# Gate multiplications held back by one result, one block in its own buffer, squares summed in a bank, 15 low parts of w_up by ScalarE and adding transfers

## The chip, the cores and the metric

The kernel runs on one core of one Trainium2 chip. The metric is the device time of one execution in microseconds (us): the time before is 820.95 us, the median of three runs (820.51 to 821.41).

## The reference

One decoder layer on 512 tokens (T) of 1024 channels (D), all in float32:

```python
u = rmsnorm(x);  proj = u @ w_in        # glu, q, k, v, r, low-rank decay, gates A and B
c = silu(layernorm(causal_conv31(a * sigmoid(g))));   y_conv = c @ w_conv_out
o = gated_linear_attention(q, k, v, decay);  o = rmsnorm(o) * silu(r);  y_gla = o @ w_gla_out
h = x + (sigmoid(gate_a) * y_conv + sigmoid(gate_b) * y_gla) @ w_o
z = causal_conv3(rmsnorm(h) @ w_ffn_up)              # 2 x 2816 channels
out = rmsnorm(h + (silu(z_a) * z_b) @ w_ffn_down)
```

## The kernel before

**Products.** TensorE (PE) multiplies in a reduced float32 format, so every operand is split into a high part and a low part (`whi`, `wlo` for weights; `uh`, `ul` and other pairs for activations), and every product is three matmuls (`mm3`, lines 527 to 529; for w_up the first of the three reads `wlo`, the two others `whi`). The weights come in tiles of 128x1024 float32 (512 KB) by transfers from the SP queue into one of four `raw` buffers. `split_weight` then makes the parts, each from a ring of four buffers: ScalarE (ACT) copies `raw` into `whi` (lines 412 and 442). For `wlo` there are three ways:

- VectorE (DVE) subtracts `whi` from `raw` (lines 413 and 450);
- for tiles listed in `ADDED`, ACT writes `raw` times -1 rounded to the reduced format, into `wlo` (line 444), and a transfer from the POOL (GpSimd) queue that adds to its destination brings the same weights from DRAM once more (line 445), so that what the rounding left off stays in `wlo`;
- for two tiles, POOL subtracts.

**Order.** The program is one list of weight tiles (`order`), and `LOOK = 2` tiles are made ready ahead of the one in use. Some pairs of products are done with seven block products in place of eight ("two" and `SEVEN`): their operands are sums of weight blocks, which POOL makes with `two_sums` (line 384, parts x1 and x3) or DVE with line 360 (`kept`), and PE's partial results are put together by DVE (`r`, line 1535, or `tmp`, line 1335). Engines run their own instructions in the order in which the program gives them, and wait for each other at semaphores.

**Around the r gate (w_r, about 225 to 290 us).** The columns r of w_in go through the steps a11, a12, s1, n2, s4, n3, a22 (`seven`), each with two blocks d = 0 and 1. `put_r` takes each result out of PSUM: the first ones into `r` buffers (ring of 8), later ones by a DVE sum or difference in place (line 1535); when a result is final, ACT applies Silu (line 1536) and DVE multiplies it into the attention output `ot` (line 1537; in the profile `h<-h,r`, since `ot` lies in buffers of the name h). The last block of w_r, step a22 with d = 1, is loaded into a `raw` buffer (line 346); behind it in SP's queue are the two blocks of the first pair of w_gb (line 292), whose sums POOL makes.

**Around the LayerNorm of the convolution (about 310 to 335 us).** `ln_center(k)` for eight channel tiles subtracts the mean on DVE (line 1015, `c`), squares on ACT (line 1017) and adds the square to a running sum on DVE (line 1021). The running sum is in an SBUF buffer `btmp`. PSUM banks of the name ax are three.

**Feed-forward (about 465 us to the end).** w_up has 44 tiles; 28 of them are used plain (the numbers in the change are among theirs), 16 in eight pairs. The low parts of all plain tiles are made by DVE (line 450). POOL makes the pairs' sums (line 384), and from its queue go adding transfers for w_down (lines 350 and 374). ACT and DVE also take PE's results out of PSUM and do the width-3 convolution and the gate between them.

Of the kernel before, what the change touches and what calls it, by code (L numbers as in the profile page):

```python
# [10 lines left out]
F32 = mybir.dt.float32  # L11
# [4 lines left out]
ALU = mybir.AluOpType  # L16

P = 128
D = 1024
T = 512  # L20
NT = T // P
KT = D // P
# [24 lines left out]
ADDED = {("w_glu", j) for j in range(4, 2 * KT)} | {("w_qk", m) for m in range(KT)}  # L47
ADDED |= {("w_v", KT // 2 + j) for j in range(KT // 2)} | {("w_gb", m) for m in range(AHEAD)}
POOLED = {("w_qk", 0), ("w_qk", 1)}
ADDED -= POOLED  # L50
RATE = 5.0
ROWS = (0, 5, 5, 5, 8, 8, 8, 8)
EVERY = (6, 6, 6, 6, 4, 4, 4, 4)
# [47 lines left out]
def trunk_layer(ctx: ExitStack, tc: tile.TileContext, a: dict, out: bass.AP):  # L101
    nc = tc.nc
# [5 lines left out]
    def scoped(name, bufs, side="left"):  # L108
        scope = ExitStack()
        return scope, scope.enter_context(tc.tile_pool(name=name, bufs=bufs, side=side))  # L110
# [16 lines left out]
    def nm(s):  # L127
        return f"{s}_{next(names)}"
# [7 lines left out]
    def btmp():  # L136
        return tp.tile([P, T], F32, tag="btmp", name=nm("btmp"), bufs=2)
# [17 lines left out]
    def ax_bank():  # L155
        return ps.tile([P, T], F32, tag="ax", name=nm("ax"), bufs=3)
# [124 lines left out]
    def load():  # L281
        if len(raws) < len(order):
            name, j = order[len(raws)]
            if name in SEVEN:
                raws.append(load_block(name, *j))
                return
            if name == "two":
                name, p, q, part = j
                if part == "x1":
                    pair_raws[name, p] = [raw_tile() for _ in range(2)]  # L290
                    for raw, m in zip(pair_raws[name, p], (p, q)):
                        nc.sync.dma_start(raw, a[name][m])
                raws.append(None)
                return
            raw = raw_tile()
            nc.sync.dma_start(raw, a[name][j])
            raws.append(raw)
# [8 lines left out]
    def raw_tile():  # L306
        return wp.tile([P, D], F32, tag="raw", name=nm("raw"), bufs=4)


    def block(name, pairs, d, row, col):  # L310

        pairs = pairs[2 * d : 2 * d + 2]
        first = pairs[0][row]
        if name == "w_r":
            tiles = a[name][4 * col : 4 * col + 4, :, first * P : (first + 2) * P]
            return tiles.rearrange("m p c -> p m c")
        w = a[name][col * SEVEN[name] + first // 2]
        return w if len(pairs) == 2 else w[:, row * T : (row + 1) * T]

    def keep_tile(name):  # L320
        if name in ("w_o", "w_r"):
            return tp.tile([P, D], F32, tag="x", name=nm("kept"), bufs=3)
        return fp.tile([P, D], F32, tag="kept", name=nm("kept"), bufs=2)

    def shaped(name, t):
        return t.rearrange("p (m c) -> p m c", c=2 * P) if name == "w_r" else t
# [4 lines left out]
    def load_block(name, pairs, step, d):  # L331

        loads = R_LOADS if name == "w_r" else LOADS
        if step not in loads:
            return None
        at = loads[step]
        src = block(name, pairs, d, *at)
        n = D if name == "w_r" else src.shape[-1]
        if step == "a11":
            dst = keep_tile(name)[:, :n]  # L340
            kept[pairs, d] = dst
        elif (name, step, d) == ("w_r", "a22", 0):
            dst = keep_tile(name)
        else:
            dst = raw_tile()[:, :n]
        load_dma = nc.sync.dma_start(shaped(name, dst), src)
        if name == "w_down":
            tc.keep_in_program_order(load_dma)
        if step == "n3":
            nc.gpsimd.dma_start(dst, block(name, pairs, d, 1, 1), accum_op=ALU.add)  # L350
        if step in ("n2", "s1"):
            kept[pairs, d, "b22" if step == "n2" else "b12"] = dst
        return dst
# [100 lines left out]
    def prefetch(n):  # L454

        while len(ready) < min(used[0] + n, len(order)):
            split_weight()
# [10 lines left out]
    def weight(name, j, ahead=LOOK):  # L468
# [3 lines left out]
        prefetch(ahead)  # L472
        share = {"two": 2.5, "w_glu": RATE, "w_r": 2.0}.get(name, RATE)
        quiet[0] = name == "w_v"
        if name == "w_qk":
            share = 1.0 if j < 2 else RATE
        if name == "w_gb" and j > 3:
# [498 lines left out]
    stat = {}  # L976
# [36 lines left out]

    def ln_center(k):
        nc.vector.tensor_tensor(conv[k], stat["mean"], conv[k], ALU.add)
        sq = btmp()
        nc.scalar.activation(sq, conv[k], AF.Square)
        if k == 0:
            stat["sq"] = sq
        else:  # L1020
            nc.vector.tensor_tensor(stat["sq"], stat["sq"], sq, ALU.add)  # L1021

    def ln_var():
        v = small(NT, "mean")
# [27 lines left out]
    def norm_chain():  # L1052
        chain = [(RATE, ln_parts)]
        chain += [(2.5, lambda: None)] * 3
        chain.append((0, ln_mean))
        chain.extend((2, lambda k=k: ln_center(k)) for k in range(KT))
        chain += [(2.5, lambda: None)] * 4
        chain.append((RATE, ln_var))
        chain.append((2.5, lambda: None))
        chain.append((0, ln_rstd))  # L1060
        chain.extend((2.5, lambda k=k: ln_out(k)) for k in range(KT))
        return chain
# [164 lines left out]
    ot = {}  # L1227
# [180 lines left out]
    r_scope, rp_ = scoped("r", 8, "right")  # L1408
# [106 lines left out]
        def __getitem__(self, step):  # L1515
            return tuple(x[self.k] for x in merge_acts[step])

    rt = {}
    urgent += s4 + of_s4 + n3 + of_n3

    def sums_for(step):
# [2 lines left out]

    def put_r(step, t, n, acc):
        if step in ("a11", "s1", "n2"):
            rt[t, n] = rp_.tile([P, T], F32, tag="r", name=nm("r"), bufs=8)
            return nc.scalar.copy(rt[t, n], acc)
        if step == "a22":
            rt[t, n] = rp_.tile([P, T], F32, tag="r", name=nm("r"), bufs=8)  # L1530
            nc.scalar.activation(rt[t, n], acc, AF.Silu)
        else:
            r = rt[t, n]
            one, two = (r, acc) if step == "n3" else (acc, r)
            done = nc.vector.tensor_tensor(r, one, two, ALU.add if step == "a12" else ALU.subtract)
            nc.scalar.activation(r, r, AF.Silu)
        nc.vector.tensor_tensor(ot[t, n], ot[t, n], rt[t, n], ALU.mult)
        return done if step == "n3" else None

    def r_at(step, i):  # L1540
        if (step, i) == ("a22", 1):
            for m in range(4, KT):
                gated_o(m, ax_bank)

    seven("w_r", R_PAIRS, [ByTile(k) for k in range(4)], None, r_at, put=put_r, before=sums_for)
    half_of = [range(KT // 2), range(KT // 2, KT)]
    open_tiles = {}
# [282 lines left out]
    for gi, pairs in enumerate(GROUPS):  # L1830
# [26 lines left out]
        for what, i, *rest in up_plan(gi):  # L1857
# [7 lines left out]
            if what == "part":  # L1865
                if rest[0] == "x1":
                    units[i] = two_tiles("w_up", i, FT + i, lambda: up_acts, ax_bank)
                done = next(units[i])
# [112 lines left out]
```

## Time and profile before

| what | value |
|---|---|
| median of three runs | 820.95 us |
| the profiled execution | 821.88 us |
| its span, first to last instruction | 820.2 us |
| PE busy | 808.7 us (99%) |
| DVE busy | 707.2 us (86%) |
| ACT busy | 488.2 us (60%) |
| POOL busy | 196.8 us (24%) |
| granted clock of TensorE | 0.998 |

The profiled execution takes 821.88 us, of which 820.2 lie between its first and its last instruction and 1.7 around them. In the views, a row of a timeline has its start, its duration, the engine (an engine's name with q is its queue of transfers), the line, the operation and the tiles as out<-in; in brackets stands how long the engine was idle before it and what ended that. A row with x2 holds two neighbours of one kind. In the groups, the columns behind the bar are busy time, mean nanoseconds of one, and the idle time ahead of them. A matmul of 128x512 is shown with 0.39 to 0.40 us though the next starts 0.23 us behind it: they are pipelined, so starts are what to compare.

### The profile page before, as it was taken

To read this page: it belongs to the slowest core of one execution; us is meant where nothing else is said; L and a number is where in the kernel's file an instruction comes from. 1 tells how busy PE (TensorE), PEld (TensorE's weight loads), DVE (VectorE), ACT (ScalarE), POOL (GpSimd) and SP (SyncE) were. 2 spreads that over 40 slices of the span, in tenths; PEclk is the share of its full clock that TensorE was granted. 3 is DMA by queue.
4 is the path that set the end of the run, shared out by engine and by line. 5 is a ranking of instruction groups with operands and counts; after the bars stand their busy time and mean duration, and the time that the engine had idled before them with its cause. 6 is when DMAs were issued, how large, how long until landed. Compare 5 with 4: busy or idle time off the path is not lost.

```text
span 820.2 us, 11465 instructions
## 1 busy us (share of the span) xinstructions
PE 808.7 (99%) x4227; PEld 695.5 (85%) x4227; DVE 707.2 (86%) x1105; ACT 488.2 (60%) x744; POOL 196.8 (24%) x176
## 2 busy tenths in 40 slices
PE   9999999999999999999999999999999999999996
PEld 8888888888888788889988898898889988899885
DVE  6879999998999878595789889979975999689895
ACT  6667788677547574384445646556435663466554
POOL 2025433332203332122001100230123311522012
PEclk9999999999999999999999999999999999999999
DMA  8488858655831332433458613146632346335662
GB/s 327 153 193 177 190 161 178 157 123 134 183 96 36 96 111 95 129 103 103 155 106 227 201 58 103 52 159 166 140 130 92 143 121 167 103 103 178 156 129 103
DMA packets 36472, 113.60 MB, mean 139 GB/s; under 512 B 3688, under 2 KB 8944, under 8 KB 36416
## 3 DMA queue, kind: packets, MB, share of 16 engines
q1 hardware_dynamic: 28912, 86.39, 31.0%
q0 software_dynamic: 7488, 26.48, 18.9%
q8 instruction: 33, 0.54, 0.3%
q14 instruction: 23, 0.19, 0.1%
q10 hardware_dynamic: 16, 0.00, 0.0%
HBM read 110.76 MB, written 2.10 MB: 138 GB/s over the span
## 4 chain that ended last, share of the span: by engine, by line
PE 62%; DVE 1%; ACT 0%; issue 0%; POOL 0%; POOLq 0%; ACTq 0%
PE mm L527 14%; PE mm L528 14%; PE mm L529 14%; PE cv L527 4%; PE cv L528 4%; PE cv L529 4%; PE ax L529 2%; PE ax L527 2%; PE ax L528 2%; DVE btmp L1021 0%; PE ax L608 0%; PE ax L1233 0%; DVE wlo L413 0%; ACT junk L1778 0%; DVE hres L1485 0%
## 5 line engine op out<-in xcount | busy, mean ns | idle before, releaser
L527 PE MATMUL mm<-uh,wlo 128*128 128x512 f32 (+1 forms) x532 | 194.0, 365 | 0.7 <-DVE tmp L1335 0.7
L528 PE MATMUL mm<-ul,whi 128*128 128x512 f32 (+1 forms) x532 | 191.5, 360 | 0.0
L529 PE MATMUL mm<-uh,whi 128*128 128x512 f32 (+1 forms) x532 | 191.5, 360 | 0.0
L413 DVE TENSOR_TENSOR wlo<-raw,whi 128x1024 fp32r<-128x1024 f32 x82 | 96.8, 1186 | 30.4 <-ACT whi L412 26.6
L384 POOL TENSOR_TENSOR raw<-raw,raw 128x512 f32<-128x512 f32 x39 | 59.8, 1534 | 239.5 <-DVE wlo L413 107.3
L527 PEld LDWEIGHTS mm<-uh,wlo 128*128 128x128 f32 x532 | 100.5, 189 | 16.5 <-DVE tmp L1335 1.1
L529 PEld LDWEIGHTS mm<-uh,whi 128*128 128x128 f32 x532 | 100.4, 189 | 15.3
L528 PEld LDWEIGHTS mm<-ul,whi 128*128 128x128 f32 x532 | 100.5, 189 | 14.8
L442 ACT CAST whi<-raw 128x1024 fp32r<-128x1024 f32 x80 | 83.5, 1048 | 30.4 <-PE mm L529 13.3
L412 ACT CAST whi<-raw 128x1024 fp32r<-128x1024 f32 x82 | 78.9, 965 | 38.1 <-PE mm L529 23.1
L450 DVE TENSOR_TENSOR wlo<-raw,whi 128x1024 fp32r<-128x1024 f32 x50 | 66.2, 1328 | 7.2 <-ACT whi L442 7.1
L412 ACT CAST whi<-kept 128x1024 fp32r<-128x1024 f32 (+1 forms) x40 | 40.2, 1007 | 30.2 <-DVE kept L360 15.7
L413 DVE TENSOR_TENSOR wlo<-kept,whi 128x1024 fp32r<-128x1024 f32 (+1 forms) x40 | 47.9, 1201 | 5.5 <-ACT whi L412 5.5
L887 DVE SCALAR_TENSOR_TENSOR aside<-cv,pp,aside 128x255 f32<-128x255 f32 (+6 forms) x112 | 52.1, 465 | 0.0
L887 DVE SCALAR_TENSOR_TENSOR c<-aside,btmp,c 128x247 f32<-128x247 f32 (+13 forms) x93 | 52.0, 564 | 0.0
L887 DVE SCALAR_TENSOR_TENSOR c<-cv,pp,c 128x247 f32<-128x247 f32 (+13 forms) x93 | 43.2, 464 | 1.4 <-ACT c L883 1.4
L444 ACT ACTIVATE wlo<-raw 128x1024 fp32r<-128x1024 f32 x28 | 29.4, 1059 | 19.0 <-PE mm L527 19.0
L1332 ACT COPY tmp<-mm 128x256 f32<-128x256 f32 x38 | 14.1, 370 | 34.0 <-PE mm L529 33.4
L1705 DVE SCALAR_TENSOR_TENSOR tmp<-mm,pp,tmp 128x511 f32<-128x511 f32 (+1 forms) x42 | 31.0, 741 | 2.6 <-ACT tmp L1702 2.5
L1705 DVE SCALAR_TENSOR_TENSOR tmp<-tmp,pp,tmp 128x511 f32<-128x511 f32 (+1 forms) x32 | 27.8, 887 | 0.4
L384 POOL TENSOR_TENSOR raw<-raw 128x512 f32<-128x512 f32 x13 | 26.4, 2032 | 0.0
L1485 DVE TENSOR_TENSOR hres<-hres,mm 128x512 f32<-128x512 f32 (+1 forms) x37 | 24.6, 673 | 2.1 <-PE mm L529 2.0
(499 smaller groups left out, 2092.9 us busy)
## 6 DMA issues: line engine op xcount, KB each, us to landing
raw<-in_w_up_dram SPq DMA_DIRECT2D x44, 512.0 KB, 3.6
raw<-in_w_glu_dram SPq DMA_DIRECT2D x16, 512.0 KB, 5.3
raw<-in_w_down_dram SPq DMA_DIRECT2D x15, 512.0 KB, 4.1
wlo<-in_w_glu_dram POOLq DMA_DIRECT2D x12, 512.0 KB, 7.0
kept<-in_w_down_dram POOLq DMA_DIRECT2D x10, 512.0 KB, 6.2
raw<-in_w_v_dram SPq DMA_DIRECT2D x8, 512.0 KB, 5.8
raw<-in_w_qk_dram SPq DMA_DIRECT2D x8, 512.0 KB, 6.3
raw<-in_w_gb_dram SPq DMA_DIRECT2D x8, 512.0 KB, 4.5
```

The costliest lines, as they stand in the source:

```text
L384: work = nc.gpsimd.tensor_tensor(out, x, y, ALU.add)
L412: nc.scalar.copy(hi, raw)
L413: two_low[:] = [nc.vector.tensor_tensor(lo, raw, hi.bitcast(F32), ALU.subtract)]
L442: nc.scalar.copy(hi, raw)
L444: pace[0] = nc.scalar.mul(lo, raw, -1.0)
L450: pace[0] = nc.vector.tensor_tensor(lo, raw, hi.bitcast(F32), ALU.subtract)
L527: nc.tensor.matmul(acc, ll, rh, start=first, stop=False, **kw)
L528: nc.tensor.matmul(acc, lh, rl, start=False, stop=False, **kw)
L529: nc.tensor.matmul(acc, lh, rh, start=False, stop=last, **kw)
L887: nc.vector.scalar_tensor_tensor(out[:, j:], x[:, : half_t - j], w, out[:, j:], ALU.mult, ALU.add)
L1485: done = nc.vector.tensor_tensor(hres[t, n][:, c], hres[t, n][:, c], acc[:, c], op)
L1705: nc.vector.scalar_tensor_tensor(z[:, s:], acc[:, : T - s], w[j], z[:, s:], ALU.mult, ALU.add)
```

## The change

- **Gate multiplications.** `put_r` no longer issues `ot *= r` as soon as the Silu is asked for. It puts the pair into a list `gated`, and the next call issues it behind that call's DVE sum or difference. The last one (a22, t = 3) is issued at once. The ring of `r` goes from 8 to 6 buffers.
- **The last block of w_r** is loaded into a buffer of its own, `rx`, in place of a `raw` buffer.
- **Squares.** The running sum of squares starts in a bank of PSUM (`ax`), and only the last sum is written to `btmp`. The first square is written by ACT into the bank.
- **w_up.** 15 plain tiles go into `ADDED`: their `wlo` is made by ACT and an adding transfer, and no longer by DVE.

```diff
--- before.py
+++ after.py
@@ -48,6 +48,7 @@
 ADDED |= {("w_v", KT // 2 + j) for j in range(KT // 2)} | {("w_gb", m) for m in range(AHEAD)}
 POOLED = {("w_qk", 0), ("w_qk", 1)}
 ADDED -= POOLED
+ADDED |= {("w_up", j) for j in (1, 23, 3, 25, 4, 26, 8, 9, 31, 20, 35, 16, 39, 19, 41)}
 RATE = 5.0
 ROWS = (0, 5, 5, 5, 8, 8, 8, 8)
 EVERY = (6, 6, 6, 6, 4, 4, 4, 4)
@@ -341,6 +342,8 @@
             kept[pairs, d] = dst
         elif (name, step, d) == ("w_r", "a22", 0):
             dst = keep_tile(name)
+        elif (name, step, d) == ("w_r", "a22", 1):
+            dst = rp_.tile([P, D], F32, tag="rx", name=nm("rx"), bufs=1)
         else:
             dst = raw_tile()[:, :n]
         load_dma = nc.sync.dma_start(shaped(name, dst), src)
@@ -1013,12 +1016,14 @@
 
     def ln_center(k):
         nc.vector.tensor_tensor(conv[k], stat["mean"], conv[k], ALU.add)
-        sq = btmp()
+        sq = btmp() if k else ax_bank()
         nc.scalar.activation(sq, conv[k], AF.Square)
         if k == 0:
             stat["sq"] = sq
         else:
-            nc.vector.tensor_tensor(stat["sq"], stat["sq"], sq, ALU.add)
+            total = stat["sq"] if k < KT - 1 else btmp()
+            nc.vector.tensor_tensor(total, stat["sq"], sq, ALU.add)
+            stat["sq"] = total
 
     def ln_var():
         v = small(NT, "mean")
@@ -1515,7 +1520,7 @@
         def __getitem__(self, step):
             return tuple(x[self.k] for x in merge_acts[step])
 
-    rt = {}
+    rt, gated = {}, []
     urgent += s4 + of_s4 + n3 + of_n3
 
     def sums_for(step):
@@ -1524,17 +1529,26 @@
 
     def put_r(step, t, n, acc):
         if step in ("a11", "s1", "n2"):
-            rt[t, n] = rp_.tile([P, T], F32, tag="r", name=nm("r"), bufs=8)
+            rt[t, n] = rp_.tile([P, T], F32, tag="r", name=nm("r"), bufs=6)
             return nc.scalar.copy(rt[t, n], acc)
         if step == "a22":
-            rt[t, n] = rp_.tile([P, T], F32, tag="r", name=nm("r"), bufs=8)
+            rt[t, n] = rp_.tile([P, T], F32, tag="r", name=nm("r"), bufs=6)
             nc.scalar.activation(rt[t, n], acc, AF.Silu)
         else:
             r = rt[t, n]
             one, two = (r, acc) if step == "n3" else (acc, r)
             done = nc.vector.tensor_tensor(r, one, two, ALU.add if step == "a12" else ALU.subtract)
             nc.scalar.activation(r, r, AF.Silu)
-        nc.vector.tensor_tensor(ot[t, n], ot[t, n], rt[t, n], ALU.mult)
+        if step == "a22":
+            done = None
+        with tc.issue_after(done.ins) if done else ExitStack():
+            while gated:
+                i, j = gated.pop()
+                nc.vector.tensor_tensor(ot[i, j], ot[i, j], rt[i, j], ALU.mult)
+        gated.append((t, n))
+        if (step, t, n) == ("a22", 3, 0):
+            i, j = gated.pop()
+            nc.vector.tensor_tensor(ot[i, j], ot[i, j], rt[i, j], ALU.mult)
         return done if step == "n3" else None
 
     def r_at(step, i):
```

PE's instructions are the same and in the same order (4023 rows). DVE has 1091 in place of 1106, ACT 724 in place of 709, POOL 192 in place of 177, SP 180 as before.

**DVE at the end of w_r.** `r` is a result of the gate, `h<-h,r` its multiplication, cv and mm are banks of PSUM, kept and raw are weight blocks. Before, from the last block of s4 (`r_442`, `r_443`) to the first pair of w_gb:

```order
L1535 TENSOR_TENSOR r_442_2605<-mm_405_2426,r_442_2605 128x512
L1537 TENSOR_TENSOR h_345_2140<-h_345_2140,r_442_2605 128x512
L413 TENSOR_TENSOR wlo_449_2661<-kept_333_2078,whi_448_2660 128x1024
L1535 TENSOR_TENSOR r_443_2619<-mm_406_2427,r_443_2619 128x512
L413 TENSOR_TENSOR wlo_453_2670<-kept_351_2153,whi_452_2669 128x1024
L1537 TENSOR_TENSOR h_346_2142<-h_346_2142,r_443_2619 128x512
L1535 TENSOR_TENSOR r_434_2563<-r_434_2563,cv_403_2424 128x512
L1537 TENSOR_TENSOR h_347_2144<-h_347_2144,r_434_2563 128x512
L1535 TENSOR_TENSOR r_435_2577<-r_435_2577,mm_404_2425 128x512
```

Now:

```order
L1540 TENSOR_TENSOR r_442_2604<-mm_405_2426,r_442_2604 128x512
L1547 TENSOR_TENSOR h_254_1619<-h_254_1619,r_420_2480 128x512
L416 TENSOR_TENSOR wlo_449_2660<-kept_333_2078,whi_448_2659 128x1024
L1540 TENSOR_TENSOR r_443_2618<-mm_406_2427,r_443_2618 128x512
L1547 TENSOR_TENSOR h_345_2140<-h_345_2140,r_442_2604 128x512
L416 TENSOR_TENSOR wlo_453_2669<-kept_351_2153,whi_452_2668 128x1024
L1540 TENSOR_TENSOR r_434_2562<-r_434_2562,cv_403_2424 128x512
L1547 TENSOR_TENSOR h_346_2142<-h_346_2142,r_443_2618 128x512
L1540 TENSOR_TENSOR r_435_2576<-r_435_2576,mm_404_2425 128x512
L1547 TENSOR_TENSOR h_347_2144<-h_347_2144,r_434_2562 128x512
```

The multiplication of each result (`h_345` for `r_442`, `h_346` for `r_443`) stands one result later, so `h_346` moves from ahead of `r_434<-r_434,cv_403`, which frees the bank cv, to behind it; ahead of it there is now `h_345`, which stood earlier.

In SP's queue, `rx` is loaded ahead of the blocks of w_r that need a `raw` buffer, and the w_gb pair has no block of w_r directly ahead of it that must wait for a third buffer; DVE's sum of `kept_351` with that block, which stood between the low parts of `raw_416` and `raw_380`, stands two low parts earlier.

**DVE at the sums of squares.** L1021 (before) and L1025 (now) are the sums, c the subtraction of the mean, L1335 and L1340 the putting together of a pair of products, for whose banks PE waits. Before:

```order
L413 TENSOR_TENSOR wlo_532_3137<-raw_503_2948,whi_531_3136 128x512
L1414 TENSOR_TENSOR h_359_2237<-mm_525_3072,h_359_2237 128x512
L1021 TENSOR_TENSOR btmp_517_3024<-btmp_517_3024,btmp_534_3143 128x512
L413 TENSOR_TENSOR wlo_537_3177<-raw_528_3089,whi_536_3176 128x1024
L1021 TENSOR_TENSOR btmp_517_3024<-btmp_517_3024,btmp_535_3147 128x512
L1335 TENSOR_TENSOR tmp_512_3012<-tmp_512_3012,mm_508_3008 128x256
L1335 TENSOR_TENSOR tmp_512_3012<-cv_509_3009,tmp_512_3012 128x256
L450 TENSOR_TENSOR wlo_542_3202<-raw_533_3140,whi_541_3201 128x1024
```

Now:

```order
L1025 TENSOR_TENSOR ax_517_3024<-ax_517_3024,btmp_530_3094 128x512
L416 TENSOR_TENSOR wlo_532_3137<-raw_503_2948,whi_531_3136 128x512
L1025 TENSOR_TENSOR ax_517_3024<-ax_517_3024,btmp_534_3143 128x512
L1018 TENSOR_TENSOR c_270_1688<-ax_516_3020,c_270_1688 128x512
L1419 TENSOR_TENSOR h_359_2237<-mm_525_3072,h_359_2237 128x512
L1018 TENSOR_TENSOR c_314_1951<-ax_516_3020,c_314_1951 128x512
L1340 TENSOR_TENSOR tmp_512_3012<-tmp_512_3012,mm_508_3008 128x256
L1025 TENSOR_TENSOR ax_517_3024<-ax_517_3024,btmp_535_3147 128x512
L416 TENSOR_TENSOR wlo_537_3177<-raw_528_3089,whi_536_3176 128x1024
L1340 TENSOR_TENSOR tmp_512_3012<-cv_509_3009,tmp_512_3012 128x256
L1025 TENSOR_TENSOR btmp_540_3187<-ax_517_3024,btmp_539_3185 128x512
```

The first of the two `tmp_512` rows stood behind the sum of `btmp_535` and the low part `wlo_537`; it now stands ahead of both, and the sum reads and writes the bank `ax_517`.

**POOL and ACT in the feed-forward.** On POOL, before, the four sums of one pair of w_up (x1: three rows, x3: one) and the first two of the next:

```order
L384 TENSOR_TENSOR raw_1136_6632<-raw_1130_6600,raw_1131_6601 128x512
L384 TENSOR_TENSOR raw_1136_6632<-raw_1136_6632,raw_1131_6601 128x512
L384 TENSOR_TENSOR raw_1131_6601<-raw_1131_6601 128x512
L384 TENSOR_TENSOR raw_1136_6632<-raw_1136_6632,raw_1130_6600 128x512
L384 TENSOR_TENSOR raw_1161_6790<-raw_1153_6737,raw_1154_6738 128x512
L384 TENSOR_TENSOR raw_1161_6790<-raw_1161_6790,raw_1154_6738 128x512
```

Now, with the adding transfers of tiles 35 (`wlo_1150`) and 16 (`wlo_1164`):

```order
L387 TENSOR_TENSOR raw_1137_6643<-raw_1131_6611,raw_1132_6612 128x512
L387 TENSOR_TENSOR raw_1137_6643<-raw_1137_6643,raw_1132_6612 128x512
L387 TENSOR_TENSOR raw_1132_6612<-raw_1132_6612 128x512
L387 TENSOR_TENSOR raw_1137_6643<-raw_1137_6643,raw_1131_6611 128x512
L448 DMA wlo_1150_6698<-in_w_up_dram 128x1024
L387 TENSOR_TENSOR raw_1162_6802<-raw_1154_6749,raw_1155_6750 128x512
L387 TENSOR_TENSOR raw_1162_6802<-raw_1162_6802,raw_1155_6750 128x512
L387 TENSOR_TENSOR raw_1155_6750<-raw_1155_6750 128x512
L448 DMA wlo_1164_6839<-in_w_up_dram 128x1024
```

Tile 35's transfer stands behind the x3 sum of its pair; tile 16's ahead of the x3 sum of the next.

On ACT, around tile 39, before and now (L442 and L445 are its high part, L447 its multiplication by -1, L1724 and L1738 a copy of an activation's high part):

```order
L1332 COPY tmp_1219_7115<-mm_1216_7112 128x256
L442 COPY whi_1224_7163<-raw_1204_7069 128x1024
L1724 COPY ah_1208_7081<-f_1205_7071 128x512
L1332 COPY tmp_1220_7116<-mm_1216_7112 128x256
L1724 COPY sh_1210_7085<-v_1207_7077 128x768
```

```order
L1337 COPY tmp_1220_7128<-mm_1217_7125 128x256
L445 COPY whi_1225_7176<-raw_1205_7082 128x1024
L1738 COPY ah_1209_7094<-f_1206_7084 128x512
L447 ACTIVATE wlo_1226_7177<-raw_1205_7082 128x1024
L1337 COPY tmp_1221_7129<-mm_1217_7125 128x256
L1738 COPY sh_1211_7098<-v_1208_7090 128x768
```

The multiplication of tile 39 stands behind the copy of `ah`, not beside the high part.

## The prediction

> **What bounds the kernel now.** I read the page's first part, then PE's waits, then the timelines around each wait.
>
> ```profile
> span 820.2 us, 11465 instructions
> PE 808.7 (99%) x4227; PEld 695.5 (85%) x4227; DVE 707.2 (86%) x1105; ACT 488.2 (60%) x744; POOL 196.8 (24%) x176
> ```
>
> PE is busy in 99% of the span, and the change leaves every instruction of PE as it is. So the time changes only where PE waits. The view of waits for PE is short:
>
> ```profile
> engine line waited for: us in total, times, longest us
> PE cv L527 <- DVE r L1535: 1.5, 1, 1.5
> PE mm L647 <- DVE ones L620: 1.1, 1, 1.1
> PE ax L1233 <- DVE h L1241: 1.0, 1, 1.0
> PE mm L527 <- DVE tmp L1335: 0.7, 1, 0.7
> ```
>
> The second stands at the program's start and isn't touched. The others are what the first three parts of the change can win, 3.2 us by this view. None lies in the feed-forward, where PE's groups from 478 to 810 us show no idle time (the largest of them; the last number is its idle time):
>
> ```profile
> L527 PE MATMUL mm<-uh,wlo 128*128 128x512 f32 (+1 forms) x232 | 82.2, 354 | 0.0
> ```
>
> So relief of DVE there is worth nothing by itself, and a low part that comes later than its first matmul costs its whole delay.
>
> **Wait on r (stall 1).** PE's starts and DVE's rows around it:
>
> ```profile
> 278.92 0.39 PE L529 MATMUL mm<-whi,sumsq 128*128 128x512 f32 x1
> 280.79 0.47 PE L527 MATMUL cv<-whi,ul 128*128 128x512 f32 x1 [1.49 <-DVE r L1535]
> ```
> ```profile
> 276.04 0.68 DVE L1535 TENSOR_TENSOR r<-mm,r 128x512 f32<-128x512 f32 x1
> 276.64 1.72 DVE L413 TENSOR_TENSOR wlo<-kept,whi 128x1024 fp32r<-128x1024 f32 x1
> 278.28 1.77 DVE L1537 TENSOR_TENSOR h<-h,r 128x512 f32<-128x512 f32 x1
> 279.97 0.67 DVE L1535 TENSOR_TENSOR r<-r,cv 128x512 f32<-128x512 f32 x1
> ```
> ```profile
> 273.74 3.53 POOL L384 TENSOR_TENSOR raw<-raw,raw 128x512 f32<-128x512 f32 x2 [14.86 <-DVE h L1537]
> 277.24 2.26 POOL L384 TENSOR_TENSOR raw<-raw 128x512 f32<-128x512 f32 x1
> ```
> ```profile
> 288.34 0.68 DVE L1537 TENSOR_TENSOR h<-h,r 128x512 f32<-128x512 f32 x1
> ...
> 330.38 1.21 DVE L450 TENSOR_TENSOR wlo<-raw,whi 128x1024 fp32r<-128x1024 f32 x1
> ```
> ```profile
> 265.88 3.95 SPq L292 DMA_DIRECT2D raw<-in_w_gb_dram  x2
> ```
>
> While POOL adds, DVE's operations with two SBUF inputs take longer (1.77 against 0.68, 1.72 against 1.21); the one that reads PSUM does not (0.68). The held-back order by itself wins nothing here: between `r_443` and the subtraction from cv there is still one multiplication and one low part, only `h_345` instead of `h_346`. What wins is that POOL is done. Its sums wait for the second of the two w_gb blocks; the row of SP's queue is 265.88 to 269.83, so the second issue stands near 269.5, behind a buffer that the last w_r block held. With `rx` it can go right behind the first, about 3 us earlier, and the sums then end near 276.5, not 279.50. Then from 276.04: starts 0.60 + 0.60 + 1.14 later, and the subtraction ends near 279.1, not 280.64. PE would have started at 279.15. I take **-1.5** (bounds: -0.8, if the sums come only half as early; -1.65, the start-to-start gap of 1.87 less the matmul's step of 0.23).
>
> **Wait on h (stall 2).** In front of line 1241 the low part, the held multiplication and the order stay, and all of it moves with PE. I take **0** (bounds: 1.0 either way, the wait itself: gone, or as much again for PE's transposes, which now find `h_348` one low part later).
>
> **Wait on tmp (stall 3).**
>
> ```profile
> 324.48 1.38 DVE L1021 TENSOR_TENSOR btmp<-btmp,btmp 128x512 f32<-128x512 f32 x1
> 325.79 2.32 DVE L413 TENSOR_TENSOR wlo<-raw,whi 128x1024 fp32r<-128x1024 f32 x1
> 328.02 1.77 DVE L1021 TENSOR_TENSOR btmp<-btmp,btmp 128x512 f32<-128x512 f32 x1
> 329.72 0.41 DVE L1335 TENSOR_TENSOR tmp<-tmp,mm 128x256 f32<-128x256 f32 x1
> ```
> ```profile
> 329.07 0.39 PE L529 MATMUL mm<-oa,whi 128*128 128x512 f32 x1
> 330.18 0.39 PE L527 MATMUL mm<-uh,wlo 128*128 128x256 f32 x1 [0.73 <-DVE tmp L1335]
> ```
>
> PE waits 1.11 - 0.23 = 0.88 us for the first combination, which stood behind 4 us of sum and low part. In the new order it comes ahead of both, and the sums read a bank, the kind of operation that POOL did not slow above. What it reads is long there: the last to come, by the wait above, is DVE itself. I take **-0.85** (bounds -0.7 to -0.9); next in line is the second combination, 0.41 us behind. The added bank is one of three ax banks, held until the last sum; a PE product that wanted it would wait for one sum, 0.7 to 1.4 us. PE shows no wait for an ax bank in that stage now, and I leave it at nothing (bound: 1.4).
>
> **15 low parts: what they cost.** Each subtraction leaves DVE and comes back as an ACT multiplication and a transfer:
>
> ```profile
> L450 DVE TENSOR_TENSOR wlo<-raw,whi 128x1024 fp32r<-128x1024 f32 x50 | 66.2, 1328 | 7.2 <-ACT whi L442 7.1
> L444 ACT ACTIVATE wlo<-raw 128x1024 fp32r<-128x1024 f32 x28 | 29.4, 1059 | 19.0 <-PE mm L527 19.0
> wlo<-in_w_glu_dram POOLq DMA_DIRECT2D x12, 512.0 KB, 7.0
> ```
>
> DVE loses 15 x 1.33 = 20 us, ACT gains 15 x 1.06 = 16 us: both beside PE. What counts is that 1.3 us of DVE become 1.06 of ACT and then a transfer of 5.3 to 9.2 us. The DMA view answers for single adding transfers of 512 KB: in the window 223 to 224 us one that is issued alone, from 183 to 185 one that runs into a crowd of others, and from 127.8 to 128.3 one that is issued together with one load:
>
> ```profile
> wlo<-in_w_gb_dram POOLq DMA_DIRECT2D x1, 512.0 KB, 5.3
> ```
> ```profile
> wlo<-in_w_gb_dram POOLq DMA_DIRECT2D x1, 512.0 KB, 9.2
> ```
> ```profile
> raw<-in_w_qk_dram SPq DMA_DIRECT2D x1, 512.0 KB, 3.5
> wlo<-in_w_qk_dram POOLq DMA_DIRECT2D x1, 512.0 KB, 8.0
> ```
>
> **Tile 35.** Before, around its first matmul:
>
> ```profile
> 704.84 2.21 POOL L384 TENSOR_TENSOR raw<-raw,raw 128x512 f32<-128x512 f32 x1 [2.36 <-DVE wlo L413]
> ```
> ```profile
> 707.08 1.26 SPq L292 DMA_DIRECT2D raw<-in_w_up_dram  x2
> ```
> ```profile
> 712.08 0.40 PE L527 MATMUL cv<-uh,wlo 128*128 128x512 f32 x1
> ```
>
> Its transfer stands in POOL's queue behind this x3 sum. With DVE's subtraction gone from beside it the sum may take 1.3 us, not 2.2: issue near 706.2. But the two loads of 512 KB behind that sum then start at the same moment. At 8.0 us the low part lands at 714.2, and PE wants it at 712.08: **+2.1** (bounds: 0 at 5.3 us, +3.3 at 9.2).
>
> **Tile 39.**
>
> ```profile
> 748.68 0.63 ACT L1724 CAST ah<-f 128x512 fp32r<-128x512 f32 x1 [1.34 <-DVE f L1719]
> ```
> ```profile
> 750.89 0.90 SPq L346 DMA_DIRECT2D kept<-in_w_down_dram  x2
> ```
> ```profile
> 756.98 0.40 PE L527 MATMUL mm<-uh,wlo 128*128 128x512 f32 x1
> ```
>
> Its multiplication stands behind the `ah` copy: 749.3 to 750.35, transfer issued at 750.4, with two loads of w_down half a microsecond behind and one of w_up beside it. Between 8.0 and 9.2 I take the middle, 8.6: landing 759.0, **+2.0** (bounds: 0 at 5.3, +2.6 at 9.2).
>
> **The narrow ones.** Tile 16 stands for 8, 9 and 20 too:
>
> ```profile
> 717.87 1.05 ACT L442 CAST whi<-raw 128x1024 fp32r<-128x1024 f32 x1 [3.76 <-PE ax L529]
> ```
> ```profile
> 724.75 0.40 PE L527 MATMUL mm<-uh,wlo 128*128 128x512 f32 x1
> ```
>
> The multiplication takes the place of this copy, the transfer goes at 718.8, and alone it lands at 724.1, 0.6 us early; a load 1.4 us behind it may take that. For the four I take **+0.6** in all (bounds 0 and +2, 0.5 each). The other nine transfers can be issued 8 us or more ahead of their first matmuls, counted in the same way, and cost nothing.
>
> **The sum:** -1.5 + 0 - 0.85 + 2.1 + 2.0 + 0.6 = **+2.35 us** on the profiled execution's 821.88. That one lies 0.93 above the median of 820.95; on the median it is 820.95 + 2.35 = 823.3.
>
> [...]
>
> **Rivals.**
> - **All transfers hidden (faster).** If loads on SP's queue hardly delay an adding transfer, it lands in 5.3 to 5.6 us: tile 35 at 711.8, tile 39 at 756.0, both ahead of PE by under 1 us. It decides at a latency of 5.9 for tile 35 and 6.6 for tile 39. For it speaks the row of 5.3 us; against it the row of 8.0, where one load was enough, and here there are two and three. Then 820.95 - 2.35 = 818.6. [...]
> - **One of the two late.** Tile 35's loads may be issued a little later than its transfer, or tile 39's: 820.95 - 2.35 + 0.4 + 2.0 = 821.0.
> - **Wins don't come.** If the w_gb sums don't move (SP's queue may hold them for another buffer), stall 1 stays, since the order itself wins nothing; with both tiles late 820.95 - 0.85 + 4.7 = 824.8, and 825.6 if the combination is held by the bank too. This is also the case that the change doesn't do what it says.
>
> **Chances.** Forecast 0.47, all hidden 0.28, one late 0.15, wins missing 0.10. By over 0.2% (1.64 us, about what a measurement of this kernel tells from no change) faster is below 819.3, slower above 822.6. The forecast's own range, 821 to 826, puts a third of it within: 0.31 slower, 0.16 same. So faster 0.28 + 0.02 = 0.30, same 0.16 + 0.13 = 0.29, slower 0.31 + 0.10 = 0.41. The range goes from 818.2, past the hidden case, to 826.2, past the missing wins; under 0.15 is left out: stalls that win more than the sums of their bounds allow with all hidden, and both tiles at 9.2 us with narrow ones late as well.
>
> **What would show it.** In the waits of PE after: the rows on DVE r and DVE tmp gone or under 0.2 us (stalls 1 and 3), the row on DVE h L1246 near 1.0; a new row of PE waiting for the adding transfer wlo<-in_w_up of about 2 us twice, at tiles 35 and 39; the DMA issues with wlo<-in_w_up x15 at a median near 6 to 7 us. POOL's w_gb sums start near 271, not 273.74. The prediction is wrong if PE waits for none of these transfers, or for far more of them than two.

## The result and the profile after

The changed kernel takes 832.73 us (median of four runs, 831.93 to 833.89) against 821.18 us for the kernel before in the same session: a ratio of 1.0136, 95% interval 1.0124 to 1.0149. It is 11.5 us slower; the forecast was 2.35. The profiled execution takes 832.84 us, 10.96 more than the one of before.

The first part of the page of the changed kernel:

```profile
span 831.1 us, 11500 instructions
PE 810.8 (98%) x4227; PEld 695.6 (84%) x4227; DVE 686.5 (83%) x1090; ACT 502.3 (60%) x759; POOL 207.5 (25%) x191
```

PE does the same work. Its busy time is up by 2.1 us all the same (810.8 against 808.7), and its idle time by 8.8 (20.3 against 11.5). The idle part is in its waits:

```profile
PE mm L530 <- DMA wlo<-in_w_up_dram: 6.4, 4, 2.9
PE cv L530 <- DMA wlo<-in_w_up_dram: 3.3, 2, 1.9
PE mm L650 <- DVE ones L623: 1.1, 1, 1.1
PE mm L744 <- ACT h L671: 0.8, 1, 0.8
PE ax L1238 <- DVE h L1246: 0.7, 1, 0.7
PE mm L530 <- ACT whi L445: 0.5, 1, 0.5
```

The rows on DVE r and DVE tmp are gone, as forecast, and six waits for adding transfers of w_up have come, 9.7 us together. The timeline has each (tiles 3, 9, 20, 35, 16 and 39 in this order; the brackets hold the idle time):

```profile
505.54 0.47 PE L530 MATMUL mm<-uh,wlo 128*128 128x512 f32 x1 [1.13 <-DMA wlo<-in_w_up_dram]
...
609.10 0.50 PE L530 MATMUL cv<-uh,wlo 128*128 128x512 f32 x1 [1.41 <-DMA wlo<-in_w_up_dram]
...
634.57 0.50 PE L530 MATMUL mm<-uh,wlo 128*128 128x512 f32 x1 [1.28 <-DMA wlo<-in_w_up_dram]
...
716.56 0.50 PE L530 MATMUL cv<-uh,wlo 128*128 128x512 f32 x1 [1.94 <-DMA wlo<-in_w_up_dram]
...
732.16 0.50 PE L530 MATMUL mm<-uh,wlo 128*128 128x512 f32 x1 [1.07 <-DMA wlo<-in_w_up_dram]
...
767.54 0.50 PE L530 MATMUL mm<-uh,wlo 128*128 128x512 f32 x1 [2.90 <-DMA wlo<-in_w_up_dram]
```

From start to start each of them costs 0.16 us more than its bracket, since the view shows a matmul 0.16 us longer than its step to the next (0.39 against 0.23): 10.7 us for the six. The busy part is in the granted clock. These are stretches of 1 to 1.5 us behind the wait at 716.56; the number behind POOL's count is the clock:

```profile
716.50:717.50 1.00, 0.94 (x4) 0.81 (x5) 0.97 (x1) 0.00 (x0) 0.64 (x1) 1.00 0.73 299
717.50:718.50 1.00, 1.00 (x6) 0.78 (x5) 0.26 (x1) 0.00 (x0) 1.00 (x1) 0.78 0.00 0
718.50:719.50 1.00, 1.00 (x4) 0.81 (x3) 0.00 (x0) 0.00 (x0) 0.92 (x2) 0.50 0.00 0
719.50:721.00 1.50, 1.50 (x6) 1.22 (x5) 0.00 (x0) 0.00 (x0) 1.50 (x2) 0.50 0.00 0
721.00:722.00 1.00, 1.00 (x9) 1.00 (x8) 0.00 (x0) 0.00 (x0) 0.48 (x1) 0.76 0.00 0
722.00:723.00 1.00, 1.00 (x10) 1.00 (x10) 0.39 (x1) 0.00 (x0) 0.00 (x0) 1.00 0.00 0
```

The clock falls to 0.50, and matmuls of 128x512 start 0.43 us apart instead of 0.23. Lost clock over these rows: 0.22 + 0.50 + 0.75 + 0.24 = 1.7 us, which at half the clock is a stretch of 3.4 us. Behind the other five waits it stayed at 1.00 in this execution.

The first half of the program gained what it should. DVE's rows at the former stall 1 (the last row frees the bank cv), then POOL's sums there:

```profile
275.36 0.68 DVE L1540 TENSOR_TENSOR r<-mm,r 128x512 f32<-128x512 f32 x1
275.96 1.18 DVE L1547 TENSOR_TENSOR h<-h,r 128x512 f32<-128x512 f32 x1
277.06 1.21 DVE L416 TENSOR_TENSOR wlo<-kept,whi 128x1024 fp32r<-128x1024 f32 x1
278.19 0.68 DVE L1540 TENSOR_TENSOR r<-r,cv 128x512 f32<-128x512 f32 x1
```
```profile
271.35 3.00 POOL L387 TENSOR_TENSOR raw<-raw,raw 128x512 f32<-128x512 f32 x2 [13.95 <-DMA raw<-in_w_gb_dram]
274.32 2.27 POOL L387 TENSOR_TENSOR raw<-raw 128x512 f32<-128x512 f32 x1
```

POOL is done at 276.6, the low part takes 1.21 us and not 1.72, and cv is free at 278.87; PE's first matmul into it starts at 279.02 without a wait in the view. At the former stall 3 the first combination has ended by 323.69, ahead of the last two sums (the first of them is shown, the other starts at 326.06):

```profile
323.27 0.42 DVE L1340 TENSOR_TENSOR tmp<-tmp,mm 128x256 f32<-128x256 f32 x1
323.61 0.69 DVE L1025 TENSOR_TENSOR ax<-ax,btmp 128x512 f32<-128x512 f32 x1
```

### The profile page after: what moved, and what is told of

Its sections match the earlier page's. It is cut to its first block, busy times and chain, and to the rows that moved or that the text cites. A ratio compares the mean times of both kernels' runs of the same rounds, so it can differ in the third digit from the quotient of the medians.

```text
span 831.1 us, 11500 instructions
## 1 busy us (share of the span) xinstructions
PE 810.8 (98%) x4227; PEld 695.6 (84%) x4227; DVE 686.5 (83%) x1090; ACT 502.3 (60%) x759; POOL 207.5 (25%) x191
## 4 chain that ended last, share of the span: by engine, by line
PE 70%; DVE 15%; DMA 7%; issue 5%; POOL 1%; ACT 1%; POOLq 0%; SPq 0%; ACTq 0%; DVEq 0%
PE mm L530 16%; PE mm L531 16%; PE mm L532 16%; DMA wlo<-in_w_up_dram 6%; DVE c L890 5%; PE cv L530 4%; PE cv L531 3%; PE cv L532 3%; DVE aside L890 3%; PE mm L744 2%; PE ax L530 2%; DVE wlo L416 2%; PE ax L532 2%; PE ax L531 2%; DMA kept<-in_w_down_dram 1%
## 5 line engine op out<-in xcount | busy, mean ns | idle before, releaser
L416 DVE TENSOR_TENSOR wlo<-raw,whi 128x1024 fp32r<-128x1024 f32 x82 | 96.5, 1184 | 46.0 <-ACT whi L415 38.4
L445 ACT CAST whi<-raw 128x1024 fp32r<-128x1024 f32 x80 | 83.6, 1049 | 18.3 <-PE mm L532 13.2
L447 ACT ACTIVATE wlo<-raw 128x1024 fp32r<-128x1024 f32 x43 | 45.4, 1061 | 36.7 <-PE mm L530 20.0
L453 DVE TENSOR_TENSOR wlo<-raw,whi 128x1024 fp32r<-128x1024 f32 x35 | 44.6, 1282 | 5.7 <-ACT whi L445 5.5
L530 PE MATMUL cv<-uh,wlo 128*128 128x512 f32 (+1 forms) x72 | 26.3, 365 | 3.3 <-DMA wlo<-in_w_up_dram 3.3
L448 POOL DMA_DIRECT2D wlo<-in_w_up_dram x15 | 13.0, 867 | 64.5 <-ACT wlo L447 59.7
```

What stands on the lines that cost most here:

```text
L416: two_low[:] = [nc.vector.tensor_tensor(lo, raw, hi.bitcast(F32), ALU.subtract)]
L445: nc.scalar.copy(hi, raw)
L447: pace[0] = nc.scalar.mul(lo, raw, -1.0)
L453: pace[0] = nc.vector.tensor_tensor(lo, raw, hi.bitcast(F32), ALU.subtract)
L530: nc.tensor.matmul(acc, ll, rh, start=first, stop=False, **kw)
```

## The experiments

The theory: PE pays every late low part in full, and nothing else in the feed-forward costs anything; the three other parts win some 2.8 us. The rivals: the adding transfers' traffic and ACT's extra work cost PE in proportion, or one of the three parts costs what another hides.

**The three parts alone.** The 15 tiles are taken out:

```diff
-ADDED |= {("w_up", j) for j in (1, 23, 3, 25, 4, 26, 8, 9, 31, 20, 35, 16, 39, 19, 41)}
```

> The changed kernel without the 15 low parts (the list ADDED as before): only the held-back multiplications, the buffer rx and the squares in a bank. Theory (the loss is in the feed-forward, the three parts win what their two stalls were): 2.5 to 3.0 us under the kernel before, no PE wait on DVE r or DVE tmp, no PE wait after 470 us. Rival (one of the three parts costs something that the 15 low parts hide): not faster than before.

Measured: 818.62 us (818.54 to 819.39) against 821.5, ratio 0.9964 (0.9951 to 0.9976). All of PE's waits that the view lists:

```profile
PE mm L649 <- DVE ones L622: 1.1, 1, 1.1
PE mm L743 <- ACT h L670: 0.8, 1, 0.8
PE ax L1237 <- DVE h L1245: 0.7, 1, 0.7
```

As expected: 2.9 us faster, nothing after 290 us. It beats both kernels, and no version here has a lower median.

**The 15 low parts alone**, on the kernel before:

```diff
 ADDED -= POOLED
+ADDED |= {("w_up", j) for j in (1, 23, 3, 25, 4, 26, 8, 9, 31, 20, 35, 16, 39, 19, 41)}
```

> The kernel before with the 15 low parts alone. Theory: 13 to 14 us over the kernel before, all of it in PE waits for adding transfers of w_up after 480 us, and the stalls on DVE r and DVE tmp as before. Rival (the two halves of the change disturb each other): near the changed kernel's time, 11 us over, or the transfers in time.

Measured: 836.26 us, ratio 1.0177 (1.0163 to 1.0191), 14.8 us slower, a little more than expected:

```profile
PE mm L528 <- DMA wlo<-in_w_up_dram: 6.6, 4, 2.8
PE cv L528 <- DMA wlo<-in_w_up_dram: 4.3, 2, 2.7
```

PE's waits had been expected to be all of it, and they are not: in the profiled execution (837.65 us) the clock stood at 0.50 from 719.3 to 726.2 us, around the wait for tile 35, and that is another 3.4 us. The two halves of the change add up within what the runs tell apart: 14.8 - 2.9 = 11.9 against the 11.5 measured.

**Nine of the 15**, without the six at which PE waited:

```diff
+ADDED |= {("w_up", j) for j in (1, 23, 25, 4, 26, 8, 31, 19, 41)}
```

> The changed kernel with nine of the 15 tiles in the list (without 3, 9, 20, 35, 16 and 39, at which PE waited). Theory (a late first matmul is the whole cost, transfers that land in time are free): 2 to 3 us under the kernel before, at most one wait of under 1 us left. Rival (the adding transfers' traffic and ScalarE's extra work cost PE in proportion to their number): 9/15 of 13.9 less 2.8, so 5 to 6 us over the kernel before.

Measured: 822.28 us, ratio 1.0007 (0.9997 to 1.0018), over ten executions from 820.21 to 823.93. Both missed: the theory by 3 us, the rival by more. The profiled execution (820.9 us) has one wait, and it is at tile 19, which was in time before:

```profile
762.57 0.50 PE L530 MATMUL mm<-uh,wlo 128*128 128x512 f32 x1 [1.36 <-DMA wlo<-in_w_up_dram]
```

Its transfer took 8.7 us among several loads and a second adding transfer. A tile that is in time only because an earlier tile made PE wait is not in time. The wide spread of the runs was not understood at this point; the experiment with tile 35 alone bears on it.

**Seven of the 15.** Tiles 19 and 41, those of the crowded end, are left out too:

```diff
+ADDED |= {("w_up", j) for j in (1, 23, 25, 4, 26, 8, 31)}
```

> The changed kernel with seven of the 15 tiles (1, 23, 25, 4, 26, 8, 31: those whose parts landed 1.9 us or more ahead of their use in every trace, and none of the crowded end). Theory (transfers in time cost nothing): the time of the three parts alone, 818.6, within 0.5 us, with no PE wait after 470 us and the granted clock at 1.00 there. Rival (each transfer costs PE something): 1 us or more over the three parts alone.

Measured: 819.10 us (818.43 to 819.78), ratio 0.9970 (0.9958 to 0.9982), 0.5 us over the three parts alone, less than the runs tell apart (their interval is 0.9951 to 0.9976). PE waits nowhere after 290 us, and the granted clock stays at 1.00 until PE is done:

```profile
PE mm L650 <- DVE ones L623: 1.1, 1, 1.1
PE ax L1238 <- DVE h L1246: 0.7, 1, 0.7
```

So seven transfers in time are free or nearly so, and they win nothing either, as PE had no wait there to win.

**A later load behind the transfer.** One more copy of `raw` into `whi`, the same values, keeps the `raw` buffer taken:

```diff
                 nc.gpsimd.dma_start(lo, a[name][spec], accum_op=ALU.add)
+                if name == "w_up":
+                    nc.scalar.copy(hi, raw)
```

> The changed kernel with one more ScalarE copy of raw into whi (the same values again) behind each of the 15 transfers, so that the raw buffer is free 1 us or more later and the next load starts later behind the transfer. Theory (a load that starts 0.56 us behind an adding transfer takes 1.4 us from it, one that starts 1.6 us behind takes next to nothing): tiles 9, 20 and 16 land 5.3 to 5.6 us after issue and no longer make PE wait, 4 us less than the changed kernel or a little more. Rival (the transfer itself takes 6.8 us at these places): the waits stay, and the time is that of the changed kernel or longer by the copies.

What the changed kernel does at tile 9 (ACT, POOL and SP's queue, then the DMA view's answer for the transfer):

```profile
600.78 1.05 ACT L447 ACTIVATE wlo<-raw 128x1024 fp32r<-128x1024 f32 x1
601.74 1.03 ACT L445 CAST whi<-raw 128x1024 fp32r<-128x1024 f32 x1
```
```profile
602.24 0.86 POOL L448 DMA_DIRECT2D wlo<-in_w_up_dram  x1 [15.11 <-ACT wlo L447]
```
```profile
602.80 0.33 SPq L297 DMA_DIRECT2D raw<-in_w_up_dram  x1
```
```profile
wlo<-in_w_up_dram POOLq DMA_DIRECT2D x1, 512.0 KB, 6.8
```

The copy into `whi` ends at 602.77, the buffer is free, and the load starts 0.56 us behind the transfer. In the experiment the load starts 2.46 us behind it:

```profile
602.29 0.86 POOL L448 DMA_DIRECT2D wlo<-in_w_up_dram  x1 [15.10 <-ACT wlo L447]
```
```profile
604.75 0.33 SPq L297 DMA_DIRECT2D raw<-in_w_up_dram  x1
```
```profile
wlo<-in_w_up_dram POOLq DMA_DIRECT2D x1, 512.0 KB, 5.5
```

At tiles 20 and 16 the same holds (load 1.6 us behind, 5.3 and 5.4 us), and the waits at all three are gone. This is as the theory has it. The time falls by some 2.2 us and not by 4, to 830.48 (ratio to before 1.0109, 1.0090 to 1.0129). One reason is that with the added copies ACT's multiplication for tile 23 runs at 492.8 us and not at 485.0, and that for tile 31 behind the copy of the high part and not ahead of it: both tiles, in time before, are now waited for. 35 and 39 still are, and tile 3 no longer is. The other is the clock: the profiled execution has two stretches of 3.4 us at 0.50, behind tiles 35 and 39, where the changed kernel's had one. PE's waits:

```profile
PE cv L532 <- DMA wlo<-in_w_up_dram: 4.0, 2, 2.7
PE mm L532 <- DMA wlo<-in_w_up_dram: 2.9, 2, 2.4
```

**The transfer in halves**, columns 0 to 511 first:

```diff
-                nc.gpsimd.dma_start(lo, a[name][spec], accum_op=ALU.add)
+                for c in (slice(0, T), slice(T, D)) if name == "w_up" else (slice(0, D),):
+                    nc.gpsimd.dma_start(lo[:, c], a[name][spec][:, c], accum_op=ALU.add)
```

> The changed kernel with each of the 15 adding transfers of w_up issued as two of 256 KB, first the left half of the columns, which PE's first four products read. Theory (what counts is when the first matmul's part lands): the first half lands 1.3 to 2 us sooner than the whole, the second in time for the fifth product 2.7 us later, and the feed-forward's waits fall from 13.9 to 3 to 6 us: 823 to 827 us. Rival (issue and receipt make up the time, not the bytes, or PE waits for both halves at once): no gain, or a loss by 15 more issues.

Measured: 826.40 us, ratio 1.0057 (1.0043 to 1.0071), 6.3 us less than the change. The 13.9 us of the expectation are the whole loss in the feed-forward, the clock's part included (10.96 and the 2.9 of the three parts). PE's waits for these transfers come down from 9.7 to 4.8 us:

```profile
PE mm L531 <- DMA wlo<-in_w_up_dram: 3.2, 3, 1.7
PE cv L531 <- DMA wlo<-in_w_up_dram: 1.6, 2, 0.9
```

The time is in the expected range, but not all of it by the way that was expected. The first halves land only 0.4 to 0.6 us sooner than the wholes at tiles 9, 20 and 16 (6.2, 6.5 and 6.4 us for 256 KB), 1.2 us sooner at 35 and 39, and 2.7 us sooner at tile 3, whose wait is gone. At 9, 20 and 16 the same load and the second half run beside them; which of the two holds them back is not shown. And the clock has a part in it: the profiled execution (825.47 us) has no stretch at 0.50. Of the four runs two, with a mean clock of 0.998 and 0.999, took 825.4 and 825.5 us, and two, with 0.996, took 827.3 and 827.6.

**Tile 35 alone.**

```diff
+ADDED |= {("w_up", j) for j in (35,)}
```

> The changed kernel with tile 35 as the only one of the 15. Theory (the wait for it is 2 us, and after such a wait the granted clock can fall to 0.5 for about 3.4 us, which costs another 1.7): 2.0 us over the three parts alone in executions with a mean clock of 0.998, 3.7 in those with a lower one, so a spread of runs of over 1.5 us. Rival (the clock after the wait at 35 comes from the other waits or the transfers around it): 2.0 us over the three parts alone with a spread like theirs, 0.9 us.

Measured: 822.62 us, ratio 1.0009 (1.0000 to 1.0018), and the runs fall into two heaps. With a mean granted clock of 0.998 they took 820.53, 820.74, 820.77, 821.16 and once 822.87 us; the seven with 0.995 or 0.996 took 822.47 to 823.51. The profiled one is of the second heap. Its wait, and the clock behind it:

```profile
712.04 0.76 PE L530 MATMUL cv<-uh,wlo 128*128 128x512 f32 x1 [2.44 <-DMA wlo<-in_w_up_dram]
712.61 0.63 PE L531 MATMUL cv<-ul,whi 128*128 128x512 f32 x1
713.03 0.63 PE L532 MATMUL cv<-uh,whi 128*128 128x512 f32 x1
```
```profile
712.00:713.00 1.00, 0.96 (x2) 0.80 (x3) 0.74 (x1) 0.00 (x0) 0.59 (x1) 0.55 0.81 332
713.00:714.00 1.00, 1.00 (x4) 0.77 (x3) 0.00 (x0) 0.00 (x0) 0.92 (x2) 0.50 0.00 0
...
716.00:718.00 2.00, 2.00 (x16) 1.88 (x15) 0.00 (x0) 0.00 (x0) 0.47 (x1) 1.00 0.00 0
```

So one late tile costs its wait, 2.1 us over the three parts alone, and in more than half of the executions 4.1; the clock's stretch is 1.7 of these 2.0 us. The spread is 3.0 us, against 0.9 for the three parts alone. As no other low part is late here, the other waits are not what makes the clock fall; the loads beside tile 35 run in the three parts alone too, where it stays at 1.00 until PE is done. The nine tiles, with one late tile, spread as widely, but not as clearly by the clock: 820.2 and 821.0 us at 0.999, 823.1 and 823.9 at 0.996, but also 823.1 and 822.4 at 0.998, so that their spread is explained in part only.

**The three parts, one at a time**, each on the kernel before: `rx` alone, with the ring of r at 6 for the space; the held-back multiplications alone, with the same ring; and the squares alone.

```diff
+        elif (name, step, d) == ("w_r", "a22", 1):
+            dst = rp_.tile([P, D], F32, tag="rx", name=nm("rx"), bufs=1)
```

> The kernel before with the buffer rx alone (the ring of r at 6, as it must be for the space). Theory (the earlier w_gb sums on POOL are what ends the wait on DVE r): 1.3 to 1.7 us under the kernel before, no PE wait on DVE r, that on DVE tmp as before. Rival (the order of the multiplications ends it): no difference over 0.3 us.

Measured: 820.55 us against 821.66, ratio 0.9988 (0.9979 to 0.9997), 1.1 us faster and a little less than expected. The wait on DVE r is down to a fifth, but not gone:

```profile
PE cv L529 <- DVE r L1537: 0.3, 1, 0.3
```

```diff
+        with tc.issue_after(done.ins) if done else ExitStack():
+            while gated:
+                i, j = gated.pop()
+                nc.vector.tensor_tensor(ot[i, j], ot[i, j], rt[i, j], ALU.mult)
+        gated.append((t, n))
```

> The kernel before with the held-back multiplications alone (ring of r at 6). Theory: within 0.4 us of the kernel before, the PE wait on DVE r near 1.5 us. Rival: 1.3 to 1.7 us faster, the wait gone.

Measured: 821.30 us, ratio 0.9993 (0.9984 to 1.0001), no difference that can be told, with the waits on DVE r and DVE h both down by 0.3 to 0.4 us in the profiled execution:

```profile
PE cv L527 <- DVE r L1535: 1.1, 1, 1.1
...
PE ax L1233 <- DVE h L1241: 0.7, 1, 0.7
```

So `rx` carries most of stall 1. Whether the order adds anything there stays open: the wait is 1.1 us with the order alone, but it is 1.2 and 1.4 in the profiles of the 15 low parts alone and the squares alone, which have neither. With both it is gone in six profiles and 0.3 in that of tile 35 alone. Stall 2 is clearer: the wait on DVE h is 0.7 us in all eight profiles with the held-back order and 1.0 in the four without.

```diff
-        sq = btmp()
+        sq = btmp() if k else ax_bank()
...
+            total = stat["sq"] if k < KT - 1 else btmp()
+            nc.vector.tensor_tensor(total, stat["sq"], sq, ALU.add)
```

> The kernel before with the sum of squares in a bank alone. Theory: 0.7 to 0.9 us under the kernel before, the PE wait on DVE tmp gone, the others as they were. Rival (the bank is missed elsewhere): a new PE wait in that stage and no gain.

Measured: 820.87 us, ratio 0.9987 (0.9979 to 0.9996), 0.8 us faster, and the wait on DVE tmp is gone. PE has no new wait in that stage, so the bank is missed nowhere there.

## Why the prediction was wrong, point by point

The frame held: PE's waits are most of the story, the first half gains, the feed-forward pays, and tiles 35 and 39 are late. The sign was right, and the time was 9 us past the forecast and outside the range. Of the signs that were named, POOL's sums did start at 271.35 and the two rows did go, but six tiles were waited for and not two, and the transfers' median is 8.3 us and not 6 to 7.

- **Stalls 1 and 3** (forecast -1.5 and -0.85): both gone from the waits, which had 1.5 and 0.7. The three parts together measured -2.9, with 0.3 of it at stall 2, which I had at 0. That 0.3 comes with the held-back order; at stall 1, where I had said that the order wins nothing by itself, the runs don't decide it.
- **Tile 35** (forecast +2.1): issued behind the x3 sum, which took 1.29 us as said, with the loads beside it, landed 8.0 us later. 1.94 + 0.16 = 2.1. The working held, and that it came out exact is in part luck: in the three other profiles with a whole transfer at tile 35 it took 7.8 to 8.1 us, and PE waited 2.4 to 2.7.
- **Tile 39** (forecast +2.0): the place was right, the latency was not: 9.4 us, past the row of 9.2 that I had as the upper bound, so 2.90 + 0.16 = 3.1. Four loads started within 1 us of it and others behind them; the transfer of 9.2 us had two loads and two adding transfers under way at its issue, and was no upper bound for this.
- **The narrow ones** (forecast +0.6 for four, at most 0.5 each): this is the step that failed. Tiles 9, 20 and 16 cost 1.6, 1.4 and 1.2, together 4.2; only 8 was free. I read one tile for all four, and put its issue 0.1 too early even so (the copy ends at 717.87 + 1.05 = 718.92, not 718.8). I took the place of the next load from the trace of before: 720.21 for tile 16, "1.4 us behind" its transfer. But that load waits for the `raw` buffer that DVE's subtraction held (at tile 16 the subtraction ended at 720.19, at tile 9 at 606.46), and the change removes the subtraction. For tile 9 the row of before shows the load at 606.49:

```profile
606.49 0.33 SPq L296 DMA_DIRECT2D raw<-in_w_up_dram  x1
```

  After, it starts at 602.80, right behind the copy into `whi` and 0.56 us behind the transfer, which itself goes out 0.4 us behind the end of the multiplication, not at once. The trace of before has a transfer with a load 0.6 us behind it, in the window 56 to 57 us, and it took what tile 9's took:

```profile
wlo<-in_w_glu_dram POOLq DMA_DIRECT2D x1, 512.0 KB, 6.8
```

  The later-load experiment shows the rest: push the load away, and the wait is gone.
- **The other nine** (forecast 0): eight were free, tile 3 cost 1.13 + 0.16 = 1.3. It is the first of three multiplications in a row (transfers at 496.19, 498.09 and 500.02), and its transfer took 9.2 us, where PE wanted the part 8.1 us behind the issue.
- **What was not in the sum at all**: the granted clock, 1.7 us in this execution. No row of before showed it: PE's longest wait there is 1.49 us, at stall 1, and behind it the clock stayed at 1.00.
- **The sum**: -2.8 for the stalls, +10.7 for six waits, +1.7 for the clock come to +9.6 of 10.96 us. A wait of 0.5 for a high part of w_down at 699 us is 0.7 more from start to start; it comes where w_down's adding transfers land later, but the profile of the squares alone has a wait of 0.4 for DVE at the same place, so that what makes it stays open. The rest, 0.7, is not assigned. Against the forecast, the narrow tiles (3.6 more), the clock (1.7), tile 3 (1.3) and tile 39 (1.1) make 7.7 of the 8.6 us by which the profiled execution passed it.
- **The rivals.** "All hidden" had 0.28 and no support in the runs: no whole transfer in the feed-forward landed under 5.2 us, and 11 of the 15 in the changed kernel took 6.8 to 9.6. The range was too narrow on the slow side because the narrow tiles were bounded by 0.5 us each, a number that rested on the load's old place.

## What to carry to other kernels

When a change removes an instruction, ask what buffers it held: the loads that waited for them move too (tile 9's from 606.49 to 602.80 us), and the trace of before shows their old places. Slack against a transfer is to be counted with every load that the new order lets start beside it, by the crowded rows and not the lone ones (9.4 us at tile 39, against 5.3 for the transfer that was issued alone). Work taken from an engine that PE does not wait for in that stage won nothing here (seven low parts in time: 819.10 us, against 818.62 for the three parts alone), so that any part of it that arrives late is pure loss.

## What the runs showed of the hardware

A wait of PE of 1.94 us (the changed kernel) or 2.44 us (tile 35 alone) can be followed by about 3.4 us of granted clock at 0.50, a further 1.7 us. It doesn't follow each time: the wait of 2.90 us at tile 39 had none in the profiled execution. In the feed-forward of the twelve profiles, five of the seven waits of 1.9 us or more have such a stretch (in the 15 low parts alone one twice as long, 6.8 us), and none of the shorter ones, up to 1.7 us, has. In the changed kernel the clock fell 1.5 us behind the end of the wait, with tile 35 alone it was down at the first matmul. Why the stretch comes in one execution and not in the next was not shown.

When no other transfer was under way at their issue, adding transfers of 512 KB in the feed-forward took 5.2 to 5.8 us if the next load started 1.1 us or more behind them (in the changed kernel 5.3 and 5.5, with 1.23 and 1.08 us), and 6.8 to 7.3 if it started 0.56 us behind (there tiles 9, 20 and 16 with 6.8, 7.0 and 6.8). With more around them they took 8.0 us (tile 35, one load at the same time and one 0.5 us behind), 9.4 (tile 39, four loads within 1 us) and 9.2 to 11.7 (the row of three at tile 3).
